# A matmul planner that counts one product's operand as ready 6 units later

## The chip, the cores and the metric

The kernel runs on one core of one Trainium2 chip. The metric is device time in microseconds (us), the median of several runs. A core has five engines that run side by side, each with its own instruction stream in a fixed order: TensorE (PE, matmuls, writes PSUM), VectorE (DVE), ScalarE (ACT), GpSimd (POOL) and SyncE (SP, which here only issues DMAs). An instruction waits on semaphores for its operands, and what stands behind it on its engine waits with it.

## What is computed

One layer of an encoder over 2048 frames of 1024 channels: a norm, one wide input projection, three branches (latent attention, a gated MLP, and a recurrent branch called RWKV-7), gates, and an output projection. The change concerns the recurrent branch. Cut to what matters, the reference has per head (8 heads of 64 channels):

```
def step(state, inp):
    r_t, w_t, k_t, v_t, a_t, b_t = inp
    sa = einsum('bhij,bhj->bhi', state, a_t)
    state = (state * w_t[:, :, None, :] + sa[..., None] * b_t[:, :, None, :]
             + v_t[..., None] * k_t[:, :, None, :])
    return state, einsum('bhij,bhj->bhi', state, r_t)

_, ys = lax.scan(step, s0, xs)            # 2048 steps
y = layernorm(ys) + bonus
merged = sum(proj * sigmoid(g_logit));  x = x + gate * rmsnorm(merged @ w_out)
```

## The kernel before

The 2048 frames are worked in four blocks of 512. Each block has a recurrence stage, `wkv(s)`, and an attention stage, `attention(s)`. Blocks are called 0 to 3 here. Projections ("gemm" below, tiles `pd<-hh,wh` and the like) are done in pieces of 128 output columns. Each f32 product is split into three matmuls over a high and a low part (`hh,wh`, `hh,wl`, `hl,wh`; `brh` and `brl` are the parts of a branch's operand).

The recurrence is not stepped frame by frame. A block is cut into chunks of 64 frames, and within a chunk the steps become small matrix products with the inverse of a triangular matrix. In a block, four pairs of heads are worked one after the other (pair 0 to 3). For each pair:

- `project` and `prepare`: gemms, then small products. The products `pst<-ard,bk` and `pso<-vt,ak` belong here. `abc`, a copy of part of them, goes to memory and back in another layout (`md`, then `mb`).
- `inverses`: DVE builds the inverses `X` from `mb` in 31 dependent steps, 58 instructions. `X` goes to memory (`xd<-X`) and comes back into the single tile `xtb` (`xtb<-xd`, 8 DMAs). This is the operand that the change is about.
- `advance`: four products that depend on each other. The first is `pss<-Pm,xtb` (16 instructions, 32 in the trace), then `pss<-u,m`, `pss<-n,xtb` and `pss<-MB,Wm`, with DVE and ACT copies in between. Out of them come `QG` and `UV`.
- `states`: the product `pss<-UV,MB`, then 8 dependent steps over the state (`pss<-S,QG`, each followed by a DVE copy), then a normalisation on DVE, ACT and POOL that makes `Y`, its transposes `pss<-consts,Y`, and the store `yr_d<-y`.

`ahead` runs project and prepare for pair after pair, not more than about two pairs ahead. `behind` runs advance and states. A stage ends when all four pairs are done and, in blocks 1 to 3, when the output of the block before it is finished (`out<-y`). Then the attention stage loads its first queries and keys (`stg<-q_d`, `stg<-k_d`; then `qh`, `kh` on ACT and `ql`, `kl` on POOL) and starts with `pss<-kh,qh`.

The order of TensorE's instructions is fixed while the program is built. Class `Pace` is a planner with a clock of its own, `t`. Each stage is a Python generator that yields what its next matmuls need, and `run` picks among the generators the one whose needs are there earliest, with ranks for ties. `note` (line 172) gives every instruction of every engine an assumed duration and records in `wrote` when each tile is written. `ready` (line 240) looks up, for each tile in a generator's list, the assumed time at which it is there. Gemms that are not urgent (`later`) are put in where the urgent generators are not ready. The order of the other engines follows the order in which the program is written out, so it changes along with it. The planner only orders: on the chip the semaphores decide, and a matmul whose operand is not there stops TensorE.

Of the kernel before, what the change touches and what calls it, by code (L numbers as in the profile page):

```python
# [90 lines left out]
class Pace:  # L91
# [148 lines left out]
    def ready(self, th):  # L240
        t = 0.0
        for n in th[2]:
            if callable(n):
                if not n():
                    return self.INF
            elif isinstance(n, tuple):
                key, bufs = n
                if key == "d" and self.lock not in (None, th[1]):
                    return self.INF
                r = self.rings.get(key, ())  # L250
                if len(r) >= bufs:
                    for e in self.used.get(r[-bufs], {}).items():
                        t = max(t, self.after(e, "PE"))
            else:
                t = max(t, self.after(self.wrote.get(self.name(n)), "PE"))
        return t
# [50 lines left out]
def trunk(ctx, tc, io, out):  # L307
    nc = tc.nc
    pace = Pace()
    V, A, G, PE, SY = (pace.engine(e) for e in (nc.vector, nc.scalar, nc.gpsimd, nc.tensor, nc.sync))  # L310
# [21 lines left out]
    RD, RS, RT, RO = ("d", PSD), ("s", PSS), ("t", PST), ("o", 1)  # L332
# [615 lines left out]
    def wkv(s):  # L948
# [6 lines left out]
        with ExitStack() as st:  # L955
# [200 lines left out]
            def advance(hp, xd, ard, el, Pm, vt, MB, abc):  # L1156
                xt = xtb
# [21 lines left out]
                def quarters(w, x):  # L1179
                    oh = [ps(), ps()]  # L1180
                    for u in range(4):
                        for h in range(2):
                            n, cs = 2 * u + h, slice(u * P, (u + 1) * P)
                            for ri in (LO, HI):
                                ro = (HI if ri is LO else LO) if h else ri
                                PE.matmul(oh[h][ro, cs], w[ri, n, :], x(h, ri, u), start=True, stop=True)
                    return oh

                yield (RS, ("s", 2), xt, Pm)
                oh = quarters(xt, lambda h, ri, u: Pm[ri, 2 * u + h, :, :])  # L1190
                u1s = [wt("u1", "a", AB) for h in range(2)]
                V.tensor_copy(u1s[0], oh[0])
# [102 lines left out]
            def behind():  # L1295
                for i in range(4):
                    yield (lambda: i in xds,)
                    zs = []
                    pace.spawn(2, gated(i, zs))
                    bv, rest = hold.pop(i)  # L1300
                    qy = yield from advance(i, xds[i], *rest)
                    yield from states(i, zs, bv, *qy)
# [454 lines left out]
```

## Time and profile before

| | us |
|---|---|
| median of 3 runs (3093.91 to 3096.95) | 3095.43 |
| the profiled execution, whole | 3098.93 |
| its span, first to last instruction | 3096.6 |
| TensorE busy in it | 2877.7 (93%) |
| VectorE busy in it | 1714.8 (55%) |

TensorE is busy for 93% of the span and no other engine for more than 55%. So the time is TensorE's work plus the time in which it stands idle, and a change of order can only alter the idle time and the clock at which the work runs. The way to read this profile is to ask for which operand TensorE stood idle, at which place in the program, and what was in its queue ahead of and behind that place.

### The profile page before, as it was taken

To read this page: it belongs to the slowest core of one execution; us is meant where nothing else is said; L and a number is where in the kernel's file an instruction comes from. 1 tells how busy PE (TensorE), PEld (TensorE's weight loads), DVE (VectorE), ACT (ScalarE), POOL (GpSimd) and SP (SyncE) were. 2 spreads that over 40 slices of the span, in tenths; PEclk is the share of its full clock that TensorE was granted. 3 is DMA by queue.
4 is the path that set the end of the run, shared out by engine and by line. 5 is a ranking of instruction groups with operands and counts; after the bars stand their busy time and mean duration, and the time that the engine had idled before them with its cause. 6 is when DMAs were issued, how large, how long until landed. Compare 5 with 4: busy or idle time off the path is not lost.

```text
span 3096.6 us, 49478 instructions
## 1 busy us (share of the span) xinstructions
PE 2877.7 (93%) x16924; PEld 2330.6 (75%) x16924; DVE 1714.8 (55%) x4574; ACT 1235.2 (40%) x2868; POOL 598.8 (19%) x606
## 2 busy tenths in 40 slices
PE   5889988989989999999999998998899999899998
PEld 4667766777867777878877777887787677788886
DVE  6426675466257753466357653446645765356653
ACT  4325433444233433444333323454433333267641
POOL 3122232332021211131011101113100110222210
PEclk8999999989999999999999999999999999999999
DMA  7888755877766689765665578655557556844456
GB/s 270 260 273 252 223 176 164 268 237 244 231 211 196 198 252 286 223 203 173 211 210 174 167 236 266 201 164 187 160 168 243 179 158 215 263 143 134 124 183 218
DMA packets 521383, 645.84 MB, mean 209 GB/s; under 512 B 142160, under 2 KB 254892, under 8 KB 521132
## 3 DMA queue, kind: packets, MB, share of 16 engines
q1 hardware_dynamic: 520960, 642.64, 66.0%
q8 instruction: 134, 2.20, 0.3%
q14 instruction: 117, 0.96, 0.1%
q10 hardware_dynamic: 172, 0.05, 0.0%
HBM read 457.69 MB, written 184.81 MB: 207 GB/s over the span
## 4 chain that ended last, share of the span: by engine, by line
PE 59%; DVE 5%; DMA 4%; ACT 2%; issue 1%; POOL 1%; SPq 1%; POOLq 0%; DVEq 0%; ACTq 0%
PE pd L120 36%; PE pss L120 10%; PE pst L120 9%; PE pso L120 4%; DMA x<-in_x 1%; SPq L120 1%; DVE X L120 1%; DVE tx L120 0%; DMA tg<-gate_d 0%; DMA wr<-in_w_out 0%; DMA wl<-kept 0%; DMA yo<-yo_d 0%; ACT Y L120 0%; DMA xtb<-xd 0%; DMA wh<-kept 0%
## 5 line engine op out<-in xcount | busy, mean ns | idle before, releaser
L120 PE MATMUL pd<-hh,wh 128*128 128x512 f32 x1952 | 810.6, 415 | 16.7 <-ACT wh L120 6.4
L120 PE MATMUL pd<-hh,wl 128*128 128x512 f32 x1952 | 775.2, 397 | 7.8 <-POOL wl L120 5.9
L120 PE MATMUL pd<-hl,wh 128*128 128x512 f32 x1952 | 773.9, 396 | 2.8 <-DVE hl L120 1.8
L120 PEld LDWEIGHTS pd<-hh,wh 128*128 128x128 f32 x1952 | 373.3, 191 | 105.5 <-issue 13.2
L120 PEld LDWEIGHTS pd<-hh,wl 128*128 128x128 f32 x1952 | 372.2, 191 | 95.6 <-POOL wl L120 9.7
L120 PEld LDWEIGHTS pd<-hl,wh 128*128 128x128 f32 x1952 | 374.5, 192 | 71.1 <-DVE hl L120 3.6
L120 DVE TENSOR_TENSOR pw<-pst,ph 128x512 fp32r<-128x512 f32 (+2 forms) x352 | 196.3, 568 | 248.9 <-ACT ph L120 247.5
L120 ACT ACTIVATE ph<-pst 128x512 fp32r<-128x512 f32 (+2 forms) x352 | 171.5, 497 | 247.6 <-PE pst L120 211.2
L120 PE MATMUL pd<-brh,wh 128*128 128x512 f32 x576 | 252.3, 438 | 18.8 <-DVE gt L120 9.0
L120 PE MATMUL pd<-brh,wl 128*128 128x512 f32 x576 | 229.8, 399 | 0.6 <-POOL wl L120 0.6
L120 PE MATMUL pd<-brl,wh 128*128 128x512 f32 x576 | 230.2, 400 | 0.0
L120 DVE TENSOR_SCALAR_CACHE_REDUCE p<-pss 128x512 f32<-128x512 f32 (+2 forms) x320 | 191.2, 607 | 69.2 <-PE pss L120 65.2
L120 ACT ACTIVATE p<-p,nm 128x512 f32<-128x512 f32 (+3 forms) x288 | 189.7, 660 | 82.8 <-DVE nm L120 82.4
L120 POOL TENSOR_TENSOR wl<-wr,wh 128x512 fp32r<-128x512 f32 x98 | 131.2, 1341 | 435.4 <-ACT wh L120 347.5
L120 ACT ACTIVATE wh<-wr 128x512 fp32r<-128x512 f32 x162 | 101.1, 628 | 230.3 <-PE pd L120 89.0
L120 PE MATMUL pst<-consts,p 128*128 128x128 f32 x1088 | 162.4, 274 | 10.7 <-DVE za L120 5.8
L120 PE MATMUL pso<-ph,v 128*128 128x256 f32 x576 | 152.8, 288 | 0.0
L120 PEld LDWEIGHTS pd<-brh,wh 128*128 128x128 f32 x576 | 111.2, 193 | 52.3 <-issue 13.8
L120 PEld LDWEIGHTS pst<-consts,p 128*128 128x128 f32 x1088 | 128.8, 141 | 27.3 <-issue 12.0
L120 PE MATMUL pso<-pw,v 128*128 128x256 f32 x576 | 146.4, 283 | 1.2 <-DVE pw L120 1.2
L120 PE MATMUL pss<-kh,qh 96*128 96x512 f32 (+2 forms) x320 | 129.3, 404 | 18.2 <-ACT kh L120 15.2
L120 POOL TENSOR_TENSOR kl<-stg,kh 96x512 fp32r<-96x512 f32 x80 | 103.4, 1296 | 220.5 <-ACT kh L120 214.2
(295 smaller groups left out, 4820.7 us busy)
## 6 DMA issues: line engine op xcount, KB each, us to landing
wh<-kept SPq DMA_DIRECT2D x486, 256.0 KB
wl<-kept SPq DMA_DIRECT2D x486, 256.0 KB
kept<-wh SPq DMA_DIRECT2D x162, 256.0 KB
kept<-wl SPq DMA_DIRECT2D x162, 256.0 KB
wr<-in_w_in SPq DMA_DIRECT2D x120, 256.0 KB
gate_d<-gt SPq DMA_DIRECT2D x64, 256.0 KB
part_d<-gt SPq DMA_DIRECT2D x64, 256.0 KB
p<-part_d SPq DMA_DIRECT2D x64, 256.0 KB
```

What stands on the lines that cost most here:

```text
L120: r = f(*a, **k)
```

## The change

A generator may now put `("late", tile, n)` in its list: the tile then counts as there `n` units of the planner's clock after the time that the planner has for it. One place uses it: the first product of `advance` asks for `xt` (the tile `xtb`) with 6.0. Nothing is computed otherwise than before, and no instruction is added or removed.

```
             if callable(n):
                 if not n():
                     return self.INF
+            elif isinstance(n, tuple) and n[0] == "late":
+                t = max(t, self.after(self.wrote.get(self.name(n[1])), "PE") + n[2])
             elif isinstance(n, tuple):
                 key, bufs = n
...
-                yield (RS, ("s", 2), xt, Pm)
+                yield (RS, ("s", 2), ("late", xt, 6.0), Pm)
                 oh = quarters(xt, lambda h, ri, u: Pm[ri, 2 * u + h, :, :])
```

What this does to the order: all that stands ahead of the first such product stays, and nearly everything behind it is planned anew. Two places follow.

TensorE, block 0, pair 2, around the product `pss<-Pm,xtb`. `pst<-consts,sq`, `pst<-consts,v`, `pst<-ard,bk` and `pso<-vt,ak` belong to the preparation of pair 3. Before:

```order
L120 MATMUL pst<-consts,sq 128x2 x4
L120 MATMUL pd<-hh,wh 128x512
L120 MATMUL pd<-hl,wh 128x512
L120 MATMUL pd<-hh,wl 128x512
L120 MATMUL pss<-Pm,xtb 64x128 x16
```

Now:

```order
L120 MATMUL pst<-consts,v 128x128 x4
L120 MATMUL pd<-hh,wh 128x512
L120 MATMUL pd<-hl,wh 128x512
L120 MATMUL pd<-hh,wl 128x512
L120 MATMUL pst<-ard,bk 128x128 x8
L120 MATMUL pss<-Pm,xtb 64x128 x16
L120 MATMUL pso<-vt,ak 64x64 x4
L120 MATMUL pst<-ard,bk 128x128 x8
```

The product has moved back past the next pair's preparation: between the last `pso<-vt,ak` of its own pair and the product stood 90 gemm matmuls, and now stand 141 and more small products. At the other pairs it moved back by 18 to 51 gemm matmuls.

SyncE, the end of block 3's recurrence stage, up to the first load of the attention stage (`stg<-q_d`). `out<-y` finishes the output of block 2, `yr_d<-y` is the store of the last pair's recurrence, `wh` and `wl` are weights. Before:

```order
L120 DMA out<-y 128x512
L120 DMA wh<-kept 128x512
L120 DMA yg<-yr_d_366 128x512
L120 DMA wl<-kept 128x512
L120 DMA stg<-q_d_326 96x512
```

Now:

```order
L120 DMA wl<-kept 128x512
L120 DMA yr_d_366<-y 128x512
L120 DMA wh<-kept 128x512
L120 DMA wl<-kept 128x512
L120 DMA stg<-q_d_326 96x512
```

The recurrence's last store has moved behind the output's last piece: it, and not the output, now stands last ahead of the attention's loads. The same happened at the ends of blocks 1 and 2. In block 0 it was so already.

## Rows read from the trace of the kernel before

**Rows 1.** The page's head and its first part: busy time by engine.

```profile
span 3096.6 us, 49478 instructions
...
PE 2877.7 (93%) x16924; PEld 2330.6 (75%) x16924; DVE 1714.8 (55%) x4574; ACT 1235.2 (40%) x2868; POOL 598.8 (19%) x606
```

**Rows 2.** TensorE's waits: waiter, what it waited for, total us, times, longest.

```profile
PE pss L120 <- DMA xtb<-xd: 34.4, 13, 11.1
...
PE pss L120 <- ACT kh L120: 15.2, 3, 7.5
...
PE pss L120 <- DVE Y L120: 6.1, 6, 1.6
...
PE pss L120 <- POOL kl L120: 3.6, 3, 1.5
```

**Rows 3.** Timeline, TensorE: start, us, instruction, count, idle before and its releaser.

```profile
466.65 0.66 PE L120 MATMUL pss<-Pm,xtb 64*64 64x128 f32 x2 [7.13 <-DMA xtb<-xd]
...
919.17 0.66 PE L120 MATMUL pss<-Pm,xtb 64*64 64x128 f32 x2 [11.11 <-DMA xtb<-xd]
920.69 2.54 PE L120 MATMUL pss<-Pm,xtb 64*64 64x128 f32 x30 [0.86 <-DMA xtb<-xd]
...
1620.27 0.66 PE L120 MATMUL pss<-Pm,xtb 64*64 64x128 f32 x2 [3.87 <-DMA xtb<-xd]
1621.61 2.68 PE L120 MATMUL pss<-Pm,xtb 64*64 64x128 f32 x30 [0.69 <-DMA xtb<-xd]
...
2408.99 0.66 PE L120 MATMUL pss<-Pm,xtb 64*64 64x128 f32 x2 [3.69 <-DMA xtb<-xd]
2410.63 2.39 PE L120 MATMUL pss<-Pm,xtb 64*64 64x128 f32 x30 [0.99 <-DMA xtb<-xd]
```

**Rows 4.** Five stretches at half clock: us, busy by engine (count), PEclk, DMA.

```profile
1618.95:1625.76 6.81, 4.81 (x46) 3.83 (x48) 0.69 (x1) 0.60 (x1) 0.00 (x0) 0.50 0.67 179
...
sum 40.89, PE 22.86 PEld 18.32 DVE 9.57 ACT 6.00 POOL 3.09; mean PE 4.57 PEld 3.67 DVE 1.91 ACT 1.20 POOL 0.62
```

**Rows 5.** Timeline, TensorE: from the last Y to the first scores, block 0.

```profile
578.48 0.60 PE L120 MATMUL pss<-consts,Y 128*128 128x128 f32 x4
578.83 0.48 PE L120 MATMUL pd<-hh,wh 128*128 128x512 f32 x1
...
588.92 0.39 PE L120 MATMUL pd<-hh,wl 128*128 128x512 f32 x1
590.06 0.33 PE L120 MATMUL pss<-kh,qh 96*128 96x128 f32 x1 [0.75 <-ACT kh L120]
```

**Rows 6.** Timeline, TensorE: the first scores of blocks 2 and 3.

```profile
1901.20 0.80 PE L120 MATMUL pss<-kh,qh 96*128 96x512 f32 x1 [7.02 <-ACT kh L120]
...
2690.25 0.79 PE L120 MATMUL pss<-kh,qh 96*128 96x512 f32 x1 [7.45 <-ACT kh L120]
```

**Rows 7.** Timeline, SyncE: the issue of the first query load, blocks 0 and 3.

```profile
584.39 0.33 SPq L120 DMA_DIRECT2D stg<-q_d  x1
...
2682.21 0.38 SPq L120 DMA_DIRECT2D stg<-q_d  x1
```

**Rows 8.** Two stretches at half clock, around the first scores of blocks 2 and 3.

```profile
sum 20.46, PE 13.07 PEld 9.65 DVE 1.93 ACT 8.17 POOL 11.13; mean PE 6.54 PEld 4.83 DVE 0.96 ACT 4.08 POOL 5.57
```

**Rows 9.** Timeline, TensorE: last state step to Y, block 1 pair 0, block 0 pair 1.

```profile
966.54 0.44 PE L120 MATMUL pss<-S,QG 64*128 64x64 f32 x4
975.47 0.63 PE L120 MATMUL pss<-consts,Y 128*128 128x128 f32 x4 [1.46 <-DVE Y L120]
...
430.96 0.69 PE L120 MATMUL pss<-S,QG 64*128 64x64 f32 x4
443.43 0.63 PE L120 MATMUL pss<-consts,Y 128*128 128x128 f32 x4 [1.35 <-DVE Y L120]
```

**Rows 10.** Busy time of DVE on X alone, in two pairs' whole chains of steps.

```profile
882.50:912.50 30.00, 15.82 (x58) 1.00 0.64 221
1709.50:1729.00 19.50, 12.04 (x58) 1.00 0.48 149
```

More of the change, by code (lines that the diff above doesn't have):

```diff
@@ L245, in ready @@
                     return self.INF
+            elif isinstance(n, tuple) and n[0] == "late":
+                t = max(t, self.after(self.wrote.get(self.name(n[1])), "PE") + n[2])
             elif isinstance(n, tuple):
@@ L1187, in quarters @@
                     return oh
-                yield (RS, ("s", 2), xt, Pm)
+                yield (RS, ("s", 2), ("late", xt, 6.0), Pm)
                 oh = quarters(xt, lambda h, ri, u: Pm[ri, 2 * u + h, :, :])
```

## The prediction

> **What bounds the kernel now.** First the page: TensorE is busy for 2877.7 of 3096.6 us, no other engine for more than 55% [rows 1]. So I looked for TensorE's idle time, by what ended it [rows 2]. The largest entry is the operand that the change is about: TensorE waited 34.4 us in 13 pieces for the DMA `xtb<-xd`. Then I asked the timeline where these pieces lie [rows 3]. They lie at 6 of the 16 products. Four carry most of what follows: block 0 pair 2 (7.13 us, and a second piece; 8.0 together), block 1 pair 0 (11.11 and 0.86, so 12.0), block 2 pair 0 (3.87 and 0.69, so 4.6), block 3 pair 0 (3.69 and 0.99, so 4.7). Block 0 pair 3 and block 1 pair 3 have the remaining 5.2. The other ten products find the operand there. So the planner takes `X` to be back sooner than it is, at some places by more than 6 us and at most by none.
>
> Third, the clock. After these waits TensorE runs at half clock for a while: the wait of 3.87 us is followed by a stretch in which the granted clock is 0.50, that is 1.2 instead of 2.4 GHz, and five such stretches around five of the six places sum to 40.89 us [rows 3, 4]. Fourth, the ends of the recurrence stages, where the first scores of blocks 2 and 3 wait 7.02 and 7.45 us for the first keys [rows 6], because the new order changes what stands ahead of them.
>
> **The change, part by part.** Nothing is computed more or less, so the sum runs over TensorE's idle time and its clock. One gemm matmul follows the other after 0.23 us: from 578.83 to 588.92 there are 44 steps [rows 5].
>
> *The waits for `xtb`.* The new order shows how much later the product comes. From the last `pso<-vt,ak` of the same pair to the product stand, before and now, 90 and 141 gemm matmuls (block 0 pair 2), 132 and 183 (block 0 pair 3), 138 and 159 (block 1 pair 0), 135 and 177 (block 1 pair 3), 129 and 147 (pair 0 of blocks 2 and 3). At 0.23 us each this is 11.7, 11.7, 4.8, 9.7 and twice 4.1 us later. At the three pairs 0 the product also moved behind small products (16 `pst<-ard,bk` and 8 `pso<-vt,ak`), which I estimate at 2.9 us, taking one gemm step for two of them. That covers the waits of 8.0, 4.7, 0.5, 4.6 and 4.7 us, the last two with some 2.4 us to spare. Block 1 pair 0 stays short: 12.0 less 7.7 leaves 4.3. The term is 34.4 − 4.3 = **30.1 us gained**. Its bounds are 34.4 (if `X` comes sooner there) and, by the first rival, 6. At the other ten pairs the product comes 18 to 51 gemm matmuls later than it needs to; this costs nothing at the product itself, since gemms fill the place.
>
> *The clock behind these waits.* In the five stretches of half clock TensorE was busy 22.86 us [rows 4]. At full clock that work takes half, so 11.4 us come back if all five go. The stretch at block 1 pair 0 shrinks to one like that of 1618.95, with 4.81 us of work, so 2.4 stay lost. **9.0 us gained.** The Trainium skill (TensorE: Matmul & The Clock Gate, section Terms) prices a throttled time by the whole of it, times one minus the share of the clock that is passed: half of 40.89 us would be 20.4 instead of 11.4. The trace speaks against it here, since 18.0 us of these stretches are the waits themselves, which the first term already has.
>
> *The ends of the stages.* Before, the stages of blocks 1 to 3 ended with the output of the block before, and in blocks 2 and 3 the first scores then waited. Now all end with the recurrence, as block 0 did. There the trace gives the latency: `Y` ends at 579.1, the query load is issued at 584.39 (5.3 later), the scores start at 590.06 (5.7 after the issue) [rows 5, 7]. In block 3 the scores start 8.0 us after the issue [rows 6, 7], so the latency is 11.0 to 13.3 us. Between the last `Y` and the scores now stand 51, 33, 57 and 54 gemm matmuls in blocks 0 to 3: 11.7, 7.6, 13.1 and 12.4 us of cover. The waits left are 3.4 us by the short latency (all in block 1) and 8.4 by the long; I take 7, nearer the long one, since three of four blocks load as much as block 3. The key's low part follows with 3.6 us in 3 places before [rows 2]; I take two of these, 2.4. Before, it was 0.75 + 7.02 + 7.45 + 3.6 = 18.8. That gives 9.4 us gained. The two half-clock stretches there held 13.07 us of work [rows 8], so 6.5 us; one, at block 1, arises anew at 2.4. Together **13.5 us gained**, from 4 to 25.
>
> *What the product's followers lose.* Gemms that stand ahead of the product no longer stand behind it. I counted them between the steps of each pair. The thinnest is now the normalisation: from the last state step to `Y` stand 21 gemm matmuls, 4.8 us, in pair 0 of blocks 2 and 3, where 33 stood. The nearest rows are block 1 pair 0, where 8.5 us went by and TensorE waited 1.46 of them, and block 0 pair 1 with 11.8 [rows 9]. By the first, 3.7 us are lost at each of the two, by the second 7.0. I take the first, as it is a pair 0 as well: 7.4. A wait of 3.7 us brings half clock, as the 3.69 did [rows 3], at 2.4 each: 4.8. Together **12 us lost**, from 6 to 24.
>
> *All other waits.* TensorE's idle time is 3096.6 − 2877.7 = 218.9 us [rows 1]. The entries above are 59 of it. The other 160 are small pieces, in part ahead of the first moved product, where nothing changes; the rest is dealt anew. Block 0 pair 2 now has small products close on each other (see the order), and pair 1 got gemms between its states. Nothing in the rows says which way this goes: 0, give or take 12.
>
> **The sum.** 30.1 + 9.0 + 13.5 − 12 = 40.6 us less. The profiled execution took 3098.9 whole, so 3058.3; it was 3.5 above the median of the runs, so the median should be near **3055**.
>
> **The rivals.** *The operand comes later too.* `X` is built by DVE between its other work: its 58 instructions take 12.0 us of DVE in a chain of 19.5 us and 15.8 in one of 30.0 [rows 10]. The recurrence of one pair lies beside the chain of the next. If shifting it makes all chains 9.7 us longer, as this spread allows, the waits are 14 us at block 1 pair 0 and 7.3 at each pair 0 of blocks 2 and 3, 28.6 instead of 4.3, and the change does not do what it says. With 5 us of clock that is 3084. Against it: most pairs have 7 us and more to spare, and on DVE the first steps of the next chain now stand ahead of the recurrence's copies.
>
> *The cover is missing elsewhere (the slower side).* If the step from the last state to `Y` takes 11.8 us at every pair [rows 9], the gemms between them (27 to 45, 6.2 to 10.3 us, and 21 twice) leave 63 us of waits, where 6.1 before [rows 2] and 7.4 above are counted: 49 more, and the clock on top, so some 3110. It decides from a mean of some 11.3 us on (16 times that, less 126 us of cover): there the gain is gone, at 2.5 us a pair, and sooner if the clock falls too. For it: the row exists, and the planner was too hopeful with `xtb` as well. Against it: in 10 of 16 pairs TensorE did not wait for `Y` [rows 2], and the waits that there were lasted 1.6 us at most.
>
> *The whole half-clock time comes back.* If a stretch costs half its length, as a row of half clock may hide work that starts late behind it, the five give 20.4 less 3.4 instead of 9.0, and the time is 3047. This is the rule of the Trainium skill (TensorE: Matmul & The Clock Gate, section Terms) taken at its word. Against it stand the 18.0 us without work [rows 4].
>
> **How the numbers follow.** A measurement of this kernel can tell 0.2% (6.2 us) from no change, so 3089 and 3102 are the borders. Forecast (3055, itself 3035 to 3085 by the bounds above): 0.68. Operand later (3084): 0.12. Whole half-clock time (3047): 0.05. Cover missing (around 3110, or near 3095 if it takes only half of the pairs): 0.15, of which half is slower. The range leaves out the last one and the ends of the first: **3035 to 3085**. Faster 0.82 (the first three, less their upper ends), same 0.10, slower 0.08.
>
> **What would show it.** Right: waits for `xtb<-xd` under 6 us, all in block 1 pair 0; the granted clock back to 1.00 at the other places; a wait for the first keys in block 1 of 3 to 7 us, and of under 2 us in blocks 2 and 3; two waits for `Y` of about 3.7 us. Wrong: waits for `xtb` at pairs that had none, `X` chains of over 30 us, waits for `Y` in most pairs, or a sum of other small waits that grows by more than 12 us. The forecast falls if TensorE's busy time rises, since that would mean more half clock and not less.

## The result and the profile after

The changed kernel takes 3073.6 us (median of 4 runs, 3066.9 to 3078.2), the kernel before beside it 3094.7 (4 runs, 3089.8 to 3097.0). The ratio is 0.9928, 95% interval 0.9914 to 0.9943: 21 us faster by the medians, 22 by the ratio, inside the range and 18.6 us above the predicted 3055. The profiled execution took 3066.9 whole.

First the head of the page and its busy times by engine, as in [rows 1]:

```profile
span 3065.1 us, 49471 instructions
...
PE 2879.6 (94%) x16924; PEld 2331.3 (76%) x16924; DVE 1709.3 (56%) x4574; ACT 1231.8 (40%) x2866; POOL 598.2 (20%) x606
```

The span is 31.5 us shorter. TensorE's busy time is 1.9 us *longer*, so all of the gain is idle time: 3065.1 − 2879.6 = 185.5 us, where 218.9 stood.

TensorE's waits (waiter, what it waited for, total us, times, longest), the lines that answer to [rows 2] and those that grew:

```profile
PE pd L120 <- DVE gt L120: 15.2, 5, 5.5
PE pss L120 <- DVE Y L120: 11.2, 6, 3.6
...
PE pss L120 <- DVE QG L120: 6.4, 3, 3.5
...
PE pss L120 <- DVE S L120: 5.6, 8, 1.6
...
PE pss L120 <- ACT kh L120: 4.1, 2, 3.0
...
PE pss L120 <- POOL kl L120: 3.6, 4, 1.3
```

There is no line for `xtb<-xd` any more; 34.4 us of it stood there before [rows 2]. The first keys and their low parts (`kh` and `kl`) went from 18.8 to 7.7 us. `Y` went from 6.1 to 11.2. `QG`, `S` and `gt`, a gate in front of the attention stage's gemms, had less in the kernel before:

```profile
PE pd L120 <- DVE gt L120: 9.7, 7, 3.9
...
PE pss L120 <- DVE QG L120: 1.0, 3, 0.4
...
PE pss L120 <- DVE S L120: 0.3, 1, 0.3
```

The timeline of TensorE (start, us, instruction, count, idle before and its releaser) at block 0 pair 2, block 1 pair 0 and pair 0 of blocks 2 and 3, the places of [rows 3]:

```profile
485.59 1.10 PE L120 MATMUL pss<-Pm,xtb 64*64 64x128 f32 x32
...
910.67 2.02 PE L120 MATMUL pss<-Pm,xtb 64*64 64x128 f32 x31
...
1598.09 1.10 PE L120 MATMUL pss<-Pm,xtb 64*64 64x128 f32 x32
...
2370.45 1.10 PE L120 MATMUL pss<-Pm,xtb 64*64 64x128 f32 x32
```

No wait in front of the product is left. At three places all 32 instructions take 1.10 us; before, they took 3.0 to 3.4 [rows 3]. At block 1 pair 0 it is close: SyncE issues the last of the eight loads of `xtb` at 909.8 us, the product starts at 910.67 and takes 2 us at full clock, so its first instructions still stand apart, too little for the view to call it a wait.

Next, the stages. Four recurrence stages of the kernel before (each from its first `pst<-lat,w2a` to the first scores, so the wait for the first keys is in it), then its four attention stages, as sums of us and of each engine's busy time:

```profile
sum 1402.90, PE 1306.85 PEld 1013.86 DVE 845.47 ACT 475.07 POOL 237.63; mean PE 326.71 PEld 253.46 DVE 211.37 ACT 118.77 POOL 59.41
...
sum 1388.90, PE 1339.58 PEld 1138.06 DVE 742.85 ACT 665.91 POOL 294.71; mean PE 334.90 PEld 284.51 DVE 185.71 ACT 166.48 POOL 73.68
```

The same of the changed kernel:

```profile
sum 1370.20, PE 1307.98 PEld 1012.24 DVE 845.59 ACT 478.82 POOL 241.80; mean PE 326.99 PEld 253.06 DVE 211.40 ACT 119.70 POOL 60.45
...
sum 1390.00, PE 1339.94 PEld 1139.16 DVE 737.72 ACT 658.86 POOL 288.93; mean PE 334.98 PEld 284.79 DVE 184.43 ACT 164.72 POOL 72.23
```

The recurrence stages lose 32.7 us, all of it idle time (96.1 to 62.2); the attention stages stay as they were in sum. So the gain is where the change was made, and in neither kind of stage does TensorE work less long.

Last, the clock. All stretches in which the granted clock is half, summed: first the 32 of the kernel before, then the 30 of the changed one.

```profile
sum 183.97, PE 141.94 PEld 112.75 DVE 86.87 ACT 57.08 POOL 52.26; mean PE 4.44 PEld 3.52 DVE 2.71 ACT 1.78 POOL 1.63
```

```profile
sum 164.18, PE 140.17 PEld 111.74 DVE 77.84 ACT 47.62 POOL 46.22; mean PE 4.67 PEld 3.72 DVE 2.59 ACT 1.59 POOL 1.54
```

The stretches lost 19.8 us, but nearly only idle time: 141.9 us of work were done at half clock before, and 140.2 now. The forecast's clock terms (9.0 + 6.5 − 2.4 − 4.8 = 8.3 us of busy time) would have meant some 16.6 us of such work less, by the prediction's own reckoning that it takes half as long at full clock. (In the changed kernel gemm matmuls follow each other after 0.43 us in the half-clock stretch from 1177.2 us on, and after 0.23 us at full clock.) The stretches now lie elsewhere.

### The profile page after: what moved, and what is told of

Same layout as the page of the kernel before. It is cut to its first block, busy times and chain, and to the rows that moved or that the text cites. A ratio compares the mean times of both kernels' runs of the same rounds, so it can differ in the third digit from the quotient of the medians.

```text
span 3065.1 us, 49471 instructions
## 1 busy us (share of the span) xinstructions
PE 2879.6 (94%) x16924; PEld 2331.3 (76%) x16924; DVE 1709.3 (56%) x4574; ACT 1231.8 (40%) x2866; POOL 598.2 (20%) x606
## 5 line engine op out<-in xcount | busy, mean ns | idle before, releaser
L120 PEld LDWEIGHTS pd<-hh,wh 128*128 128x128 f32 x1952 | 373.8, 192 | 113.4 <-issue 18.6
L120 PE MATMUL pd<-brh,wh 128*128 128x512 f32 x576 | 250.4, 435 | 15.2 <-DVE gt L120 15.2
```

The costliest lines, as they stand in the source:

```text
L120: r = f(*a, **k)
```

## The experiments

Four questions: how far single executions scatter, whether the operand is the cause, what the number 6.0 does, and whether the waits that are left can be taken away in the same manner. "Idle" is always span less TensorE's busy time in the profiled execution.

### The same two kernels again

No edit; the changed kernel and the kernel before, each once more.

> The changed kernel once more, to see how far its runs and its profile scatter. If the ratio to the kernel before of 0.9928 holds, it lands between 0.991 and 0.995 again. Theory A (the profiled execution is typical): the profile again shows TensorE busy about 2880 us and idle for the waits named some 33 us less than before, and the ratio is nearer 0.990. Theory B (the profiled execution was a lucky one): the median stays near 3074 and this profile shows more half clock or more small waits than the first one of it.

> The kernel before once more, for a second profile of it. Theory A (the first profile of it is typical): waits for xtb within 2 us of 34.4, the sum of TensorE's idle time within 3 us of 219, TensorE busy within 3 us of 2877.7. Theory B (part of the gap between forecast and result is that the first profile was of a slow execution): idle or busy time is lower by 4 us or more, with the difference outside the waits for xtb.

The changed kernel came out at 3068.3 us, ratio 0.9926 (0.9904 to 0.9948). Its profile has the same 185.5 us of idle time, but 2883.1 us busy. The kernel before took 3090.7 in its second profiled execution: idle 214.7, busy 2873.6, waits for `xtb` 35.0. So the waits repeat within 1 us and the idle time within 4. Busy time scatters by 4 us, with the work done at half clock: 141.9 and 127.6 us before, 140.2 and 151.6 after. Between the second pair of profiles the change gives 29.2 us of idle time and takes 9.5 of busy time, 19.7 in all; between the first pair it is 31.5. The medians, 21 us apart in the first comparison and 24 in the second, lie between. So the first pair of profiles flattered the change. That is theory B in both expectations: the second profile of the changed kernel has more work at half clock and lies 2.1 us above its median, where the first lay 6.7 below (the median itself came out at 3068, not near 3074), and the second profile of the kernel before is over 4 us lower in idle and in busy time, outside the waits for `xtb`.

### An operand that is always there

Both products that read `xtb` read a block of zeros among the constants instead. TensorE's order is that of the kernel before (or, as a control, of the changed one); the inverses are replaced by zeros, so the recurrence's result is left out. A further line, not shown, tells the planner that `xtb` is read up to the same place as before, so that the order stays.

```
-                oh = quarters(xt, lambda h, ri, u: Pm[ri, 2 * u + h, :, :])
+                oh = quarters(zero, lambda h, ri, u: Pm[ri, 2 * u + h, :, :])
...
-                oh = quarters(xt, lambda h, ri, u: n1s[h][ri, u * P:(u + 1) * P])
+                oh = quarters(zero, lambda h, ri, u: n1s[h][ri, u * P:(u + 1) * P])
```

> TensorE's order is that of the kernel before, but both products that read the returned inverses read a block of zeros out of the constants in their place (the recurrence's own result is left out of the computation so). So TensorE never waits for xtb, and nothing else about its order moves. Theory A (a wait costs itself and the half clock behind it): 34.4 us of waits and some 11 us of half clock go, ratio 0.985 to 0.987, and TensorE's busy time falls to about 2866 us. Theory B (half clock is not tied to these waits, it turns up wherever small products stand close): only the waits go, busy time stays within 4 us of 2878, ratio 0.988 to 0.991. Theory C (the gain of the change comes from the ends of the stages, not from these waits): less than 12 us go, ratio over 0.996.

> The same replacement (zeros for the inverses in both products, so the recurrence's own result is left out) in the changed kernel's order, as a control. The changed kernel's profile shows no wait for xtb at all. Theories A and B: nothing to gain, the same ratio as the changed kernel in this call within 0.2%. If it is faster by more than 0.3%, the DMA or the zeros have an effect of their own, and the run noxt_before has to be read less that much.

In the order of before, 3062.7 us, ratio 0.9903 (0.9881 to 0.9926). In the order of after, 3071.7, ratio 0.9932 (0.9911 to 0.9953), which is the changed kernel itself. So the waits for `xtb` cost the old order some 30 us, and cost the new order nothing: the cause is the operand, and the change removes all of it. The control also says that the zeros gain nothing by themselves. Theory C falls, by which the ends of the stages give the gain: in the order of before they are as they were (14.2 us for `kh`, below), and 30 us go all the same. The new order seems to pay some 7 us back, though the intervals overlap.

The head of the page and the busy times of the first of the two, and its waits:

```profile
span 3069.9 us, 49412 instructions
...
PE 2875.4 (94%) x16924; PEld 2328.0 (76%) x16924; DVE 1712.3 (56%) x4574; ACT 1233.3 (40%) x2868; POOL 597.4 (19%) x606
```

```profile
PE pss L120 <- ACT kh L120: 14.2, 3, 7.6
...
PE pd L120 <- ACT wh L120: 8.8, 4, 4.0
...
PE pss L120 <- DVE Wm L120: 3.3, 1, 3.3
PE pss L120 <- ACT n L120: 3.2, 1, 3.2
```

Idle is 194.5 us: 24.4 less than before, not 34.4. With the first wait gone, the next links of the chain (`Wm`, `n`) are waited for, and the weights `wh` more than before. Busy time is 2875.4, between the two profiles of before. That is theory B: the waits go, and the clock does not come back. This is the cleanest test of the clock term: the order is the old one, the waits are gone, and the work at half clock is 146.8 us, no less than before. Where it went is in the rows. The product itself runs at full clock at all 16 places. TensorE's busy time on `Pm`, whole span, in this kernel and then in the kernel before, and last that of the kernel before within the five stretches of [rows 4]:

```profile
sum 3069.90, PE 17.66; mean PE 17.66
```

```profile
sum 3096.60, PE 29.13; mean PE 29.13
```

```profile
sum 40.89, PE 14.80; mean PE 2.96
```

The changed kernel has 19.25 in the whole span. So 10 to 11.5 us of busy time went at the product. Not all of that is clock: half of the 14.80 us is 7.4. The rest was the product standing apart between its eight loads without an idle gap that the view shows: at block 1 pair 3 of the kernel before it took 1.98 us at full clock, and where the operand was there 1.10. So order can lengthen busy time by such pauses too, beside idle time and the clock. And other stretches fell to half clock. One, block 0 pair 0, in this kernel and then in the kernel before:

```profile
354.13 6.24 PE L120 MATMUL pss<-UV,MB 128*128 128x64 f32 x30 [1.61 <-DVE QG L120]
```

```profile
351.92 3.53 PE L120 MATMUL pss<-UV,MB 128*128 128x64 f32 x30 [0.43 <-DVE QG L120]
```

The same 30 instructions, at half clock after a wait of 1.61 us and at full clock after one of 0.43.

### Six places, and other numbers

The delay of 6.0 only at the six products that waited in the kernel before, 0.0 at the other ten:

```
+    LATE = ((0, 2), (0, 3), (1, 0), (1, 3), (2, 0), (3, 0))
...
-                yield (RS, ("s", 2), ("late", xt, 6.0), Pm)
+                yield (RS, ("s", 2), ("late", xt, 6.0 if (s, hp) in LATE else 0.0), Pm)
```

> The 6 units are given only to the six products that waited in the kernel before (block 0 pairs 2 and 3, block 1 pairs 0 and 3, pair 0 of blocks 2 and 3); the other ten count their operand as before. In the order the product stands 15, 30, 21, 21, 18 and 18 gemm matmuls later at these six. Theory A: of the waits of 8.0, 4.7, 12.0, 0.5, 4.6 and 4.7 us there stay 4 to 5 and 5 us at two places, some 24 us go with 6 of half clock, but blocks 2 and 3 still end with the output of the block before, so the 15 us there stay: ratio 0.990 to 0.993. If the ten needless shifts cost something, it is faster than the changed kernel; if the ends of the stages gave much of the gain, it is slower than it by 0.2% or more.

3071.7 us, ratio 0.9934 (0.9912 to 0.9955); idle 186.4, waits for `xtb` 4.6. In sum it cannot be told from the changed kernel, so the delays at the ten products that had not waited are not needed for the gain (0.990 to 0.993 was expected). The waits are others, though: as expected, blocks 1 to 3 still end with the output of the block before, and `kh` and `kl` keep 12.6 us (7.7 in the changed kernel); `Y` has 16.5 (11.2) and `gt` 4.5 (15.2). That they come out alike in sum says nothing of a single one of them.

Then other numbers at all products:

```
-                yield (RS, ("s", 2), ("late", xt, 6.0), Pm)
+                yield (RS, ("s", 2), ("late", xt, 3.0), Pm)
```

and likewise 5.0, 7.0 and 12.0.

> 3 units in place of 6. In the order the product comes 141, 153, 147, 174, 138 and 138 gemm matmuls behind its own pair's preparation at the six places that waited (before: 90, 132, 138, 135, 129, 129; with six units: 141, 183, 159, 177, 147, 147). If the waits for xtb are what counts: some 6 to 8 us left at block 1 pair 0 and up to 2 each at pair 0 of blocks 2 and 3, ratio to the kernel before 0.993 to 0.996. If the gain with six units came from how the rest was dealt anew, late_3 can lie anywhere within 0.5% of the kernel before.

> The changed kernel with 5.0 in place of 6.0. Theory A (the gain is the waits for xtb): between the last pso<-vt,ak and the product stand 141, 171, 153 gemm matmuls at block 0 pairs 2 and 3 and block 1 pair 0, where 141, 183, 159 stood, so at most 1.5 us of waits for xtb come back; idle time within 4 us of the changed kernel's 185.5; ratio 0.991 to 0.994. Theory B (6.0 is only a lucky order): ratio anywhere from 0.990 to 0.997, with TensorE busy off by 5 us or more from 2880 to 2883.

> The changed kernel with 7.0 in place of 6.0. Theory A (waits for xtb gone, the rest as before): no wait for xtb, idle time within 4 us of 185.5, ratio 0.991 to 0.994. Theory B: ratio anywhere from 0.991 to 1.000, with TensorE busy off by 5 us or more; at 12.0 it was 2910.9 and the ratio 1.0128, so at 7.0 a rise towards 2890 would say that the loss grows with the number.

> 12 units in place of 6. No wait for xtb at any place (135 to 285 gemm matmuls ahead of the product). What it costs: the recurrence ends later in its stage, and between the last Y and the first scores stand 0, 30, 33 and 30 gemm matmuls (with six units 51, 33, 57 and 54), so the first scores should wait some 11 us in block 0 and 4 to 6 in the others, 15 to 20 us more than with six units. Theory of the waits: ratio to the kernel before 0.997 to 1.000, slower than with six units by 0.4% or more. Theory that the ends of the stages are covered by something else: within 0.2% of the six units.

| number | ratio to before (95%) | idle us | busy us | waits for `xtb` us |
|---|---|---|---|---|
| none (before) | 1 | 218.9 | 2877.7 | 34.4 |
| 3.0 | 0.9947 (0.9929 to 0.9964) | 191.8 | 2890.2 | 10.6 |
| 5.0 | 0.9941 (0.9922 to 0.9961) | 183.8 | 2892.6 | 1.4 |
| 6.0 (the change) | 0.9928 (0.9914 to 0.9943) | 185.5 | 2879.6 | none |
| 7.0 | 1.0009 (0.9994 to 1.0025) | 208.8 | 2892.9 | none |
| 12.0 | 1.0128 (1.0102 to 1.0154) | 216.0 | 2910.9 | none |

The waits for `xtb` do what was expected, down to the 1.4 us at 5.0. The time does so at 3.0, and at 5.0 on the edge (0.991 to 0.994 by theory A); busy time there is 9.5 us above the upper of the two profiles of 6.0, as theory B had it. Further up it does not: 7.0 removes as much of the waits as 6.0 and gains nothing, above theory A's range and a little above theory B's, and 12.0, for which 0.997 to 1.000 was expected, is slower than before. At 7.0, idle time is 23 us above the changed kernel's. 13 of it stand at these waits, none of which is for the operand:

```profile
PE pd L120 <- DVE gt L120: 22.6, 8, 7.7
PE pss L120 <- DVE Y L120: 12.6, 9, 4.3
...
PE pss L120 <- ACT kh L120: 8.6, 4, 4.9
```

Against the changed kernel these are 7.4, 1.4 and 4.5 us more. At 12.0 the first keys alone have 20.9 us in 5 waits, the longest 11.0, near the 15 to 20 us more that were expected of them, and busy time is 31 us up. Half of the 28 us more at half clock explains 14 of these; what the other 17 are, no run here shows.

### Taking away what is left

Three attempts with the change's own means. The first has three delays at once, and the other two one of them each (5.0 for the keys, 0.7 for `QG`):

```
-                yield (RS, ("s", 2), UV, MB)
+                yield (RS, ("s", 2), ("late", QG, 0.7), UV, MB)
...
-                yield (RS, Y, lambda: len(zs) > 0)
+                yield (RS, ("late", Y, 2.0), lambda: len(zs) > 0)
...
-                        yield (RS, qh, ql, *K[g], lambda: ...)
+                        yield (RS, qh, ql, *K[g], *([("late", K[g][0], 5.0)] if i == 0 and j == 0 and g == 0 else []), lambda: ...)
```

> The changed kernel with three more late needs: Y counts as there 2 units later for its transposes, QG 0.7 later for the product ahead of the states, and the first keys of a stage 5 later for the first scores. The profile of the changed kernel has 11.2 us of waits for Y, 6.4 for QG, 7.7 for the first keys, and stretches of half clock behind QG's waits. In the order now stand 48 gemm matmuls or so ahead of Y (36 before) save 21 at pair 0 of blocks 2 and 3, 15 to 24 ahead of the product that waits for QG (6 to 12), and 12, 45, 45 and 45 ahead of the first scores. Theory of the waits and the clock behind them: QG's waits and half of Y's go, block 0's first scores wait 8 us, in sum 10 to 15 us faster than with six units alone, ratio to the kernel before 0.987 to 0.990. Theory that each new order deals out as many new waits: within 0.2% of the changed kernel, 0.991 to 0.995.

3081.5 us, ratio 0.9959 (0.9945 to 0.9973), worse than the change alone. `Y` went from 11.2 to 7.8 and `QG` from 6.4 to 0.7, but `kh` rose to 13.8, `S` to 8.6 and `kk` to 8.0. Both ranges were missed.

> The changed kernel, and in addition the planner counts QG as there 0.7 units later ahead of UV,MB. All waits for QG (6.4 us in the changed kernel, 1.0 before) should go, and with them the half clock on the UV,MB products: their TensorE time should fall from 63.4 us back to 58 to 59. Theory A (the clock is the price of these single waits): TensorE busy 2872 to 2877, idle 178 to 182, ratio 0.988 to 0.990. Theory B (the half clock moves elsewhere): UV,MB back to 58 to 59 as well, but the whole of the work done at half clock stays between 130 and 170 us, TensorE busy 2876 to 2890, ratio 0.991 to 0.996. The cover ahead of the first scores is smaller in blocks 2 and 3 here (30 gemm matmuls, where 57 and 54 stood), so both expect 4 to 9 us more of waits for the first keys than the changed kernel had, which moves each range of idle time and ratio up by that (0.002).

3088.0 us, ratio 0.9979 (0.9968 to 0.9989). The local mechanism holds: no line for `QG` is left among its waits, and the slowest `UV,MB` instruction is at full clock again. The views of tile `UV` of this kernel and then of the changed one (ns, min/median/max):

```profile
L120 PE MATMUL pss<-UV,MB x512: 218/275/275, 370.6 to 2633.5; 128*128 128x64 f32 x171
```

```profile
L120 PE MATMUL pss<-UV,MB x512: 217/275/446, 370.0 to 2601.5; 128*128 128x64 f32 x171
```

By the same tile's busy time it fell from 65.0 us (not the 63.4 of the expectation) to 58.9. But idle is 201.3 us, 15.8 above the changed kernel, where both theories allowed 9 more at most, for the first keys:

```profile
PE pss L120 <- ACT kh L120: 16.0, 4, 4.9
PE pss L120 <- DVE S L120: 11.8, 13, 2.2
```

The 11.9 us more for `kh` come with the thinner cover (30 gemm matmuls ahead of the first scores of blocks 2 and 3 where 57 and 54 stood), as the expectation said, if by more. 3.5 us of waits for `xtb` are back. Ahead of `UV,MB` stand 348 gemm matmuls over the 16 pairs where 165 stood, and between the state steps 981 where 1017 stood; that the 6.2 more for `S` come from this thinning is argued, not shown. The work at half clock stayed at 136.8 us, busy time (2878.7) is in theory B's range, and the ratio at the upper end of its shifted one (0.993 to 0.998): the waits for `QG` went, and the time rose.

> The changed kernel, and in addition the planner counts a stage's first keys as there 5 units later. Nothing moves but the first scores of a stage: between the last Y and them now stand 51, 45, 72 and 69 gemm matmuls in blocks 0 to 3, where 51, 33, 57 and 54 stood. Theory A (the term for the ends of the stages is local: latency against cover): the waits for the first keys and their low parts, 7.7 us in the changed kernel, fall to 2 to 4 us; the wait of 3.0 us in block 1 falls by 2.8 (12 matmuls of 0.23) or goes; ratio to the kernel before 0.990 to 0.992. Theory B (the time of a new order is mostly the clock dealt anew, which no single wait decides): the waits fall just the same, but TensorE's busy time moves by several us either way, and the ratio can lie anywhere from 0.989 to 0.996.

3088.1 us, ratio 0.9978 (0.9963 to 0.9992), outside both ranges. `kh` fell from 4.1 to 1.2 but `kl` rose from 3.6 to 5.7: 6.9 us, not 2 to 4. And the time rose by 14.5 us against the changed kernel's median, the profiled span by 19.6. Most of it can be pointed at here. The row of block 0's attention stage, from its first scores to the next recurrence stage, in this kernel and then in the changed one (us, busy by engine with counts, granted clock, DMA share, GB/s):

```profile
604.00:851.20 247.20, 225.80 (x1123) 188.16 (x1121) 124.77 (x341) 95.83 (x231) 51.89 (x56) 0.92 0.73 228
```

```profile
603.40:836.20 232.80, 220.59 (x1121) 183.86 (x1120) 121.56 (x339) 95.13 (x233) 54.85 (x59) 0.95 0.78 242
```

With 1123 and 1121 matmuls it is 14.4 us longer: 9.2 more of idle time and 5.2 more of busy time, at a lower clock (0.92 and 0.95). The first scores stand where they stood (51 gemm matmuls behind the last `Y`); what changed is the order within the stage. Two of its waits, in this kernel and then the longest in the changed one:

```profile
640.88 0.79 PE L120 MATMUL pd<-brh,wl 128*128 128x512 f32 x1 [2.66 <-DVE wl L120]
...
661.43 0.80 PE L120 MATMUL pd<-hh,wh 128*128 128x512 f32 x1 [6.57 <-DVE gt L120]
```

```profile
647.32 0.47 PE L120 MATMUL pd<-brh,wh 128*128 128x512 f32 x1 [2.90 <-DVE gt L120]
```

The edit speaks of the keys, and most of the idle time lost stands 37 to 57 us behind them, at gemms that wait for a weight and for a gate. That is shown for this run. At 7.0 the same stage, with 1122 matmuls, is 12.4 us longer than at 6.0 (22.5 us of idle time where 12.2 stood). That is a third of the 36.6 us between those two profiles; that the rest has the same nature stays an argument.

## Why the prediction was right, and 19 us short

**Waits for `xtb`: right.** 30.1 us forecast, 34.4 found. The 4.3 that were to stay at block 1 pair 0 did not: the product's 910.67 lies a little behind the issue of the last load. The chain of `X` there took 28.6 us and 14.25 of DVE, against 30.0 and 15.8 in the window of [rows 10]: the chain did not become longer there. The first rival (the operand comes later too) asked for 28.6 us of waits, and with none left it falls.

**Ends of the stages, their waits: right.** 9.4 forecast, 11.1 found (18.8 to 7.7; 15.3 to 9.4 in the second pair of profiles, 5.9). The timeline at the first scores of blocks 1 and 2:

```profile
1175.23 0.50 PE L120 MATMUL pss<-kh,qh 96*128 96x512 f32 x1 [3.00 <-ACT kh L120]
...
1865.02 0.50 PE L120 MATMUL pss<-kh,qh 96*128 96x512 f32 x1 [1.15 <-ACT kh L120]
```

3.00 in block 1 (3 to 7 forecast), 1.15 in block 2 and none in block 3 (under 2 forecast); 7.02 and 7.45 stood there [rows 6].

**The followers: right in size and place.** Two waits for `Y` of 3.62 us each (3.7 forecast), in pair 0 of blocks 2 and 3, and not the 63 us of waits of the second rival: all waits for `Y` are 11.2. The rows are in the last section.

**All other waits: within the bound.** 218.9 − 185.5 = 33.4 us less idle; 34.4 + 11.1 − 5.1 are explained above, so the rest grew by 7.0 (0, give or take 12, forecast). It is `QG` (+5.4), `gt` (+5.5) and `S` (+5.3), less some others. Over all, idle time was forecast to fall by 30.1 + 9.4 − 7.4 = 32.1 us and fell by 33.4. That it is so close is in part luck: the three terms brought 4.3, 1.7 and 2.3 us more than forecast, and the rest took 7.0 of that back.

**The clock: the step that failed.** The sum had 9.0 + (6.5 − 2.4) − 4.8 = 8.3 us less of busy time; it rose by 1.9, and by 9.5 in the second pair of profiles. The prediction named that as the sign of its failure. What it said of single places was right: at none of the 16 places is the product at half clock any more, and busy time on `Pm` fell by 9.9 us (the experiments show that some 7 of that are clock). The failing step is the one that added these up as if the rest of the kernel kept its clock; the work at half clock fell by 1.8 us in its place, and rose by 24 in the second pair of profiles. `UV,MB` alone took 5.5 us back (59.45 to 64.99 by its tile). Two of its places, in the changed kernel and then in the one before:

```profile
1817.78 5.61 PE L120 MATMUL pss<-UV,MB 128*128 128x64 f32 x30 [2.27 <-DVE QG L120]
...
2595.34 6.63 PE L120 MATMUL pss<-UV,MB 128*128 128x64 f32 x30 [3.54 <-DVE QG L120]
```

```profile
1820.75 3.68 PE L120 MATMUL pss<-UV,MB 128*128 128x64 f32 x32
...
2610.42 3.68 PE L120 MATMUL pss<-UV,MB 128*128 128x64 f32 x32
```

The gemm matmuls ahead of `UV,MB` are no fewer than before at these places (9 and 12 before, 12 and 12 now), so counting them could not have found this. `QG` comes later because of what stands ahead of it on DVE. Timeline of DVE in the changed kernel, ahead of the first of the two:

```profile
1813.54 0.69 DVE L120 TENSOR_TENSOR ut<-ut,gu 128x512 f32<-128x512 f32 x1 [1.54 <-DMA ut<-sg_d]
...
1816.42 0.75 DVE L120 SCALAR_TENSOR_TENSOR y<-y,ors,x 128x512 f32<-128x512 f32 x1 [0.99 <-DMA x<-in_x]
1817.20 0.43 DVE L120 TENSOR_TENSOR QG<-pss,dg 64x256 f32<-64x256 f32 x1
```

Two instructions of other threads (one finishes the output of the block before) wait there for their DMAs, 1.54 and 0.99 us, and the pieces of `QG` wait in the queue behind them; TensorE's 2.27 us are about these. At the second place it is one such instruction, `y<-y,ors,x`, that waits 3.87 us for its DMA:

```profile
2592.88 0.75 DVE L120 SCALAR_TENSOR_TENSOR y<-y,ors,x 128x512 f32<-128x512 f32 x1 [3.87 <-DMA x<-in_x]
```

The product `UV,MB` does not itself read `QG`, and at the first place it starts while later pieces of `QG` are still to come (the last ends at 1819.2). By the code what it needs is a PSUM tile that those pieces read first; that is read from the code and not shown by a run. In the kernel before, the pieces of `QG` followed each other at both places with no such wait between. The prediction looked at TensorE's queue for each step and at DVE's for none but `X`.

The third rival, by which even more of the clock would come back (3047), falls with this step; the Trainium skill (TensorE: Matmul & The Clock Gate, section Terms) prices a throttled time by its whole length. The 19.8 us that it became shorter would be 9.9 us by that, as an estimate; the trace does not agree, since the work in it fell by 1.8 us and busy time rose.

**Profile against median: the other half of the miss.** The sum for the profiled execution was 3058.3 and it took 3066.9: 8.6 us more, which is the clock term's 10.2 (8.3 + 1.9) less the 1.3 that idle time gave beyond the forecast, to within half a us of time outside the span and roundings. The other 10.2 us come from the last step, which took the profiled execution to lie 3.5 us above the median. That was so for the profile of before; the profile of after lies 6.7 *below* its median. One profiled execution of this kernel is not placed against its median better than some 7 us.

## What to carry to other kernels

When a planner takes an operand to be there too early, the waits for it are a safe thing to look for: move the reader back by the shortfall and they go, and the trace before gives about their worth (34 us of waits, of which taking away the operand alone gave 30). But each such edit has everything behind it planned anew, which here cost up to 25 us more (7.0 against 6.0, with the same waits gone), so try neighbouring values before believing in one. Do not add the clock behind a removed wait to the gain, unless you can say that nothing else on that engine is about to wait.

## What the runs showed of the hardware

*The work at half clock moved and did not vanish.* In the fourteen profiles TensorE did 128 to 171 us of work at half clock, and no removed wait brought it below. Its busy time less half of that work is 2807 to 2810 us in ten of them: before 2877.7 − 71.0 and 2873.6 − 63.8, after 2879.6 − 70.1 and 2883.1 − 75.8, with 5.0 2892.6 − 82.2, with 7.0 2892.9 − 85.6, 2888.5 − 80.8 and 2878.7 − 68.4 with the delays for the keys and for `QG`, 2882.7 − 76.0 with the zeros in the new order, and 2888.4 − 79.2 with the six places. So between these the differences in busy time are the clock. It is not so in all: the zeros in the order of before give 2802.0, 3.0 gives 2805.0, the three delays together 2815.4, and 12.0 gives 2826.7. There the order changed busy time by something else, of which the runs show only the pauses between the loads of `xtb`.

*The same wait can end in either clock.* The two waits for `Y` in the changed kernel are alike to 0.01 us, and the same instructions follow. Timeline of TensorE, block 2 and block 3:

```profile
1646.53 0.63 PE L120 MATMUL pss<-consts,Y 128*128 128x128 f32 x4 [3.62 <-DVE Y L120]
1647.09 1.13 PE L120 MATMUL pst<-lat,w2a 64*128 64x512 f32 x4
```

```profile
2418.89 0.63 PE L120 MATMUL pss<-consts,Y 128*128 128x128 f32 x4 [3.62 <-DVE Y L120]
2419.45 1.93 PE L120 MATMUL pst<-lat,w2a 64*128 64x512 f32 x4
```

In block 3 the granted clock fell to half behind it (2419.6 to 2423.0) and the four `pst<-lat,w2a` took 1.93 us; in block 2 it did not fall, and they took 1.13. The prediction gave both of them 2.4 us of clock; one had 3.4 us of work at half clock, 1.7 by the same reckoning, and the other none. On the other side, 30 `UV,MB` fell to half clock after 1.61 us of waiting, as shown above. So the length of the wait alone does not decide; what does, these runs leave open.
